# A two-block transformer kernel: the second block's projections token major from float32r parts, a shorter Fourier transform, modulation rows shared between engines, scores issued one unit further ahead

## The chip, the cores and the metric

One core of one Trainium2 chip runs the whole program. The metric is the device time of one execution in microseconds (us); lower is better. Before the change three runs took 1713.85, 1714.11 and 1716.21 us, median 1714.11.

## The reference, cut to what matters

256 tokens of width 1024 pass through a first block (attention, convolution, a mixture of 64 experts), then through a second block of two layers. The change touches the mixer of the second block's first layer:

```
xn   = rms_norm(h) * (1 + sc1) + sh1            # 256 x 1024
proj = xn @ w_in                                # 512 Fourier, 512 q, 128 k, 128 v columns
q, k = apply_rope(q), apply_rope(k)             # pairs (2j, 2j+1) turned by cos, sin of the position
attn = softmax(q k^T / 8 over window, context, sink) v
four = real(fft2(f_in, over tokens and over each head's 128 columns))
h    = h + g1 * (concat(four, attn) @ w_out)
h    = h + g2 * swiglu(rms_norm(h) * (1 + sc2) + sh2)
```

sh1, sc1, g1, sh2, sc2, g2 are six rows of 1024 of silu(c) @ ada_w + ada_b. The mixer needs rows 2 (g1), 3 (sh2) and 4 (sc2) while it runs; rows 0 and 1 were made in the first block. All inputs and outputs are f32.

## The kernel before, in words

Activations lie feature major: eight tiles of 128 features by 256 tokens. The first block ends with sixteen quads of experts, whose weights stream from memory. Weights pass through a ring of six slots of 2 MB (`wslot`, line 441), all issued on SP's queue in the order of the program.

The second block's mixer is built by `even` (line 1809). It issues the loads (kv2, late tables, q, f, modulation row 2, output weights, modulation rows 3 and 4), normalises with `norm_mod` (line 724), and then weaves four chains in a fixed order of preference: `attention2`, `gemvs2`, `projections`, `second_out`. `weave` (line 478) asks a model of the engines (`_Model`, line 271) when each chain's next piece can run, and lets the first chain that is ready put its instructions down; so the order on TensorE, VectorE and ScalarE is written out by the program. GpSimd's order is left to the scheduler. Every instruction passes through a helper, line 264, and so carries that line in the profile; the names of the tiles tell them apart.

- `projections` (line 1746): keys feature major, then values token major, then four query tiles and four Fourier tiles feature major, each eight f32 matmuls with 256 columns, stationary weights, moving tokens (`h`). After each key or query tile `rope` (line 1636) copies it (ScalarE), multiplies it with a swap matrix (TensorE) and combines with cos and sin (three VectorE operations).
- `fourier` and `dft` (lines 1651 and 1661): per head two matmuls with the 128-point cosines and sines for each of two token tiles, a copy, and four matmuls with the 256-point tables.
- `attention2` (line 1727): eight units (head pair i, query tile qt). `scores2` (line 1682) makes one unit's scores (`ps<-kall,qT`), subtracts from the mask with a running minimum (VectorE, reads PSUM), takes the exponential (ScalarE), and normalises half on VectorE and half on GpSimd. `attend2` (line 1707) turns the probabilities (`ps<-firstt,p`), copies them (ScalarE, `p2T`) and multiplies with the values (`ps<-p2T,vall`). Scores are issued one unit ahead: in turn u the scores of unit u + 1 are put down first, then the attending of unit u. The PSUM tags are of few banks: g 3, n 1, s 2, t 1, o 1.
- `gemvs2` (line 1770) makes modulation rows 2, 3 and 4 with `gemv` (line 639): on VectorE one multiply and seven multiply-adds of 1024 columns (`acc`), then four small matmuls with ones, a copy and two transposes.
- `second_out` (line 1777): the output projection, eight tiles of eight f32 matmuls; it waits for all projections, for modulation row 2 and for the first seven tiles of `mix`.

The feed-forward layers after it (`ffn_hidden`, line 1851) already work with parts: `split2` (line 1845) rounds a weight chunk to float32r on ScalarE (`whi`) and subtracts on VectorE or GpSimd (`wlo`), the activations are split too, and three float32r matmuls (high by high, high by low, low by high) stand for one in f32.

## Time and profile before

| | |
|---|---|
| median of three runs | 1714.11 us |
| the profiled execution's own time | 1714.49 us |
| its span, first to last instruction | 1712.7 us |
| mean granted TensorE clock | 0.897 of full speed |
| busy: TensorE, VectorE, ScalarE, GpSimd | 79%, 34%, 22%, 8% of the span |
| memory traffic | 589.49 MB, mean 344 GB/s |

The rows further below come from this one execution. Times in them are us from the span's start unless marked ns. A matmul in f32 is recorded as two instructions, one in float32r as one. `x16` is a count of instructions; the text in square brackets is the idle time of the engine just before, and what ended it. PE is TensorE, DVE VectorE, ACT ScalarE, POOL GpSimd.

### The profile page before, as it was taken

The page shows a single profiled execution, that of the slowest core. Times are in us where ns is not written, and L with a number is a line of the kernel's source. Part 1 is how long each engine was busy: PE and PEld are TensorE (multiplying, and loading weights), DVE is VectorE, ACT ScalarE, POOL GpSimd, SP SyncE. Part 2 cuts the span into 40 slices and gives each one's busy share as a digit, 9 for nine tenths or more (in the row PEclk, how much of TensorE's full clock was granted, in tenths as well). Part 3 has the DMA queues.
Part 4 walks back from the last instruction along what each step waited for, and adds up shares of the span by engine and source line. Part 5 has one row for each costly group of instructions (what it writes and reads, how often), then busy time and mean ns, then how long its engine had stood idle before and what let it go on. Part 6 is the DMA issues. An engine that isn't in the chain of part 4 may idle for free.

```text
span 1712.7 us, 18392 instructions
## 1 busy us (share of the span) xinstructions
PE 1348.3 (79%) x7664; PEld 782.8 (46%) x7664; DVE 575.8 (34%) x1109; ACT 375.6 (22%) x704; POOL 143.0 (8%) x80
## 2 busy tenths in 40 slices
PE   7999976665775765667666766769989999999997
PEld 5676832221221221222122212226667778778886
DVE  1567721110110111011011101115575878464533
ACT  2335110000000000100000000013324444554444
POOL 0000000000000000000000000002202232213224
PEclk9999998878888787888888778889999999999999
DMA  9787889999999999899999999996486786636620
GB/s 396 301 344 307 320 348 427 427 427 427 428 426 427 427 427 425 368 427 426 426 427 427 426 428 427 426 426 281 163 317 236 310 342 244 246 148 232 234 74 25
DMA packets 43994, 589.49 MB, mean 344 GB/s; under 512 B 4888, under 2 KB 5016, under 8 KB 7552
## 3 DMA queue, kind: packets, MB, share of 16 engines
q1 hardware_dynamic: 42768, 584.82, 82.5%
q0 software_dynamic: 704, 2.64, 0.4%
q8 instruction: 62, 1.02, 0.2%
q10 hardware_dynamic: 432, 0.79, 0.1%
q14 instruction: 28, 0.23, 0.0%
HBM read 587.16 MB, written 1.06 MB: 343 GB/s over the span
## 4 chain that ended last, share of the span: by engine, by line
PE 30%; DMA 24%; DVE 3%; ACT 1%; issue 1%; ACTq 0%; DVEq 0%
PE ps L264 30%; DMA w<-in_w 23%; DMA w<-in_w2last 1%; DVE acc L264 1%; DMA w<-in_ada 0%; DVE wlo L264 0%; DVE p L264 0%; ACT p L264 0%; DVE x L264 0%; DVE sqa L264 0%; ACT rstd L264 0%; DVE ada L264 0%; DVE mix L264 0%; ACT mix L264 0%; ACT sq L264 0%
## 5 line engine op out<-in xcount | busy, mean ns | idle before, releaser
L264 PE MATMUL ps<-w,xg 128*32 128x512 f32 x2016 | 301.3, 733 | 186.6 <-DMA w<-in_w 186.6
L264 PE MATMUL ps<-w,gT 128*32 128x512 f32 x1024 | 175.8, 821 | 104.9 <-DMA w<-in_w 96.9
L264 PEld LDWEIGHTS ps<-w,xg 128*32 128x32 f32 x2016 | 64.2, 122 | 404.7 <-DMA w<-in_w 209.8
L264 ACT ACTIVATE whi<-w 128x1024 fp32r<-128x1024 f32 x132 | 139.4, 1059 | 151.6 <-PE ps L264 146.0
L264 DVE TENSOR_TENSOR g<-g,ps 128x512 f32<-128x512 f32 x16 | 11.0, 687 | 458.1 <-PE ps L264 458.1
L264 DVE TENSOR_TENSOR wlo<-w,whi 128x1024 fp32r<-128x1024 f32 x88 | 114.7, 1311 | 111.6 <-ACT whi L264 111.4
L264 PE MATMUL ps<-whi,mix 128*128 128x512 f32 x352 | 140.1, 403 | 4.1 <-ACT mix L264 4.1
L264 DVE SCALAR_TENSOR_TENSOR acc<-w,sil,acc 128x1024 f32<-128x1024 f32 x98 | 141.8, 1447 | 2.6 <-DMA w<-in_ada 1.1
L264 POOL TENSOR_TENSOR wlo<-w,whi 128x1024 fp32r<-128x1024 f32 x44 | 112.6, 2570 | 349.9 <-ACT whi L264 293.0
L264 PE MATMUL ps<-wlo,mix 128*128 128x512 f32 x352 | 140.4, 400 | 0.0
L264 PE MATMUL ps<-whi,xl 128*128 128x512 f32 x352 | 138.5, 399 | 0.9 <-DVE xl L264 0.9
L264 PEld LDWEIGHTS ps<-w,gT 128*32 128x32 f32 x1024 | 32.9, 131 | 230.9 <-DMA w<-in_w 151.7
L264 DVE COPY y<-ps 128x512 f32<-128x512 f32 x16 | 11.1, 692 | 279.3 <-PE ps L264 279.3
L264 ACT ACTIVATE gT<-ps 128x512 f32<-128x512 f32 x16 | 9.6, 597 | 320.0 <-PE ps L264 320.0
L264 PE MATMUL ps<-hT,w 128*128 128x256 f32 x320 | 75.7, 383 | 2.4 <-DVE hT L264 2.4
L264 PEld LDWEIGHTS ps<-whi,mix 128*128 128x128 f32 x352 | 67.4, 192 | 22.1 <-ACT mix L264 5.3
L264 DVE SCALAR_TENSOR_TENSOR x<-ps,mod,x 128x256 f32<-128x256 f32 x152 | 67.2, 483 | 28.4 <-PE ps L264 28.4
L264 PEld LDWEIGHTS ps<-whi,xl 128*128 128x128 f32 x352 | 67.3, 191 | 16.6 <-DVE xl L264 1.7
L264 PEld LDWEIGHTS ps<-wlo,mix 128*128 128x128 f32 x352 | 67.5, 192 | 14.6 <-DVE wlo L264 0.4
L264 PE MATMUL ps<-wlo,gh 128*128 128x512 f32 x176 | 69.7, 399 | 0.0
L264 PE MATMUL ps<-oh,xtok 128*128 128x128 f32 x512 | 62.6, 283 | 8.7 <-DVE oh L264 8.7
L264 PE MATMUL ps<-whi,gl 128*128 128x512 f32 x176 | 69.2, 397 | 0.0
(304 smaller groups left out, 1497.5 us busy)
## 6 DMA issues: line engine op xcount, KB each, us to landing
w<-in_w SPq DMA_DIRECT2D x189, 2048.0 KB, 26.2
w<-in_ada SPq DMA_DIRECT2D x34, 2048.0 KB, 10.1
w<-in_f SPq DMA_DIRECT2D x32, 2048.0 KB, 8.3
w<-in_wout SPq DMA_DIRECT2D x4, 2048.0 KB, 8.6
w<-in_win SPq DMA_DIRECT2D x3, 2048.0 KB, 25.1
w<-in_conv SPq DMA_DIRECT2D x4, 1536.0 KB, 11.6
w<-in_ada1h SPq DMA_DIRECT2D x2, 2048.0 KB, 14.2
w<-in_cw SPq DMA_DIRECT2D x2, 2048.0 KB, 18.3
```

Of the source, the lines that this page charges most:

```text
L264: r = f(*args, **kw)
```

## The change

Six things change, all in the second block's first mixer.

1. The projections are token major: stationary token tiles, moving weights. Both are split into float32r parts: `norm_mod` writes a high and a low part of the input, `half` splits a weight chunk of 1024 columns (ScalarE the high part, VectorE and GpSimd half of the low part each), through four buffers of a pool that was there before. `tm_gemm` runs three float32r matmuls per token tile and 128 inputs. Keys and values come first, then all of q, then the Fourier input.
2. The rope works on token-major tiles without a swap matrix, then `turned` transposes keys and queries.
3. The Fourier transform takes the tokens first, with 129 cosine and 127 sine columns only, and makes the other half of the outputs from sums and differences.
4. `gemv_shared`: four of a modulation row's eight slices are scaled on ScalarE and added on GpSimd, four stay on VectorE; the matmuls with ones add both sums.
5. Scores are issued two units ahead.
6. The masks are fetched by GpSimd's DMAs instead of being copied from the late table, which shrinks from 1088 KB to 512 KB; the model's costs for float32r matmuls and GpSimd are lowered.

The core of the diff (the packing of the inputs and the tables are left out):

```diff
...
+    def half(self, w, c):
...
+        src = w[:, D * c:D * c + D]
+        hi, lo = [self.xtra.tile([P, D], F32R, tag="x", name=self.nm(n)) for n in ("whi", "wlo")]
+        nc.scalar.activation(hi, src, AF.Copy)
+        for eng, s in ((nc.vector, slice(0, 512)), (nc.gpsimd, slice(512, D))):
+            eng.tensor_tensor(lo[:, s], src[:, s], hi[:, s].bitcast(F32), ALU.subtract)
+        return hi, lo
...
+    def tm_gemm(self, ps, chunks, cols):
...
+        m = D // cols
+        for c in chunks:
+            yield from self.ahead_half(c + 1)
+            ws = self.halves[c]
+            for kk in range(m):
+                k = m * (c - chunks[0]) + kk
+                yield self.ready(ws[1][:, cols * kk:cols * kk + cols], self.hl[:, k, :])
+                for t in range(2):
+                    st = slice(P * t, P * t + P)
+                    hi, lo = [x[:, cols * kk:cols * kk + cols] for x in ws]
+                    self.mm(ps[t][:, :cols], lhsT=self.hh[:, k, st], rhs=hi, start=k == 0, stop=False)
+                    self.mm(ps[t][:, :cols], lhsT=self.hh[:, k, st], rhs=lo, start=False, stop=False)
+                    self.mm(ps[t][:, :cols], lhsT=self.hl[:, k, st], rhs=hi, start=False, stop=k == KT - 1)
+                yield self.clock
+            yield from self.ahead_half(c + 2)
...
+    def rope(self, src, t, scale):
...
+        q = self.wk(512, "ada")[:, :n]
+        nc.scalar.activation(q, src, AF.Copy, scale=scale)
+        r = self.ph(512, "rt", 1)[:, :n]
...
+        nc.vector.tensor_tensor(pairs(r), pairs(q)[:, :, :, ::-1], sin[:, None].to_broadcast([P, n // 64, 32, 2]), ALU.mult)
+        nc.vector.tensor_tensor(qh, qh, cos[:, None].to_broadcast([P, n // 64, 64]), ALU.mult)
+        nc.vector.tensor_tensor(q, q, r, ALU.add)
+        return q
...
+    def fourier(self, i, f):
...
         for t in range(2):
+            self.mm(pz[:, :S], lhsT=f[:, t, P * i:P * i + P], rhs=self.late("dft")[:, S * t:S * t + S],
+                    start=t == 0, stop=t == 1)
+        z = self.ph(S, "fz", 2)
+        nc.scalar.activation(z, pz[:, :S], AF.Copy)
...
+        self.mm(po[:, :129], lhsT=cs[:, :P], rhs=z[:, :129], start=True, stop=True)
+        self.mm(po[:, S:S + 127], lhsT=cs[:, P:], rhs=z[:, 129:], start=True, stop=True)
...
     def attention2(self):
...
-            for n in ((0, 1) if u == 0 else (u + 1,)):
+            for n in ((0, 1, 2) if u == 0 else (u + 2,)):
...
     def projections(self):
...
+        ps = yield from self.grab("g", 2)
+        yield from self.tm_gemm(ps, (0, 1), S)
+        k = []
+        for t in range(2):
+            nc.vector.tensor_copy(self.vall[:, 0, t, :], ps[t][:, P:S])
+            k.append(self.rope(ps[t][:, :P], t, 1.0))
...
+        ps = yield from self.grab("g", 2)
+        yield from self.tm_gemm(ps, (2, 3, 4, 5), 512)
+        q = [self.rope(ps[t], t, 0.125) for t in range(2)]
...
+        self.spawn(self.turned(q, [self.qT[:, :, P * t:P * t + P] for t in range(2)], [f"q{i}" for i in range(4)]))
+        ps = yield from self.grab("g", 2)
+        yield from self.tm_gemm(ps, (6, 7, 8, 9), 512)
...
+    def turned(self, src, outs, names):
+        for x, o in zip(src, outs):
+            yield self.ready(x)
+            yield self.room("n")
+            pt = self.ps("n")
+            n = o.shape[1]
+            for i in range(n):
+                self.tr(pt[:, P * i:P * i + P], x[:, P * i:P * i + P])
+            self.nc.vector.tensor_copy(o, pt[:, :P * n].rearrange("p (i s) -> p i s", i=n))
...
+    def gemv_shared(self, slots, c, bias, out):
...
+        t0 = yield from self.take(slots, 0)
+        for k in range(4):
+            nc.scalar.activation(t0[:, k, :], t0[:, k, :], AF.Copy, scale=c[:, k:k + 1])
+            yield self.model.clock["scalar"] - BACKLOG
+            if k % 2:
+                nc.gpsimd.tensor_tensor(t0[:, k - 1, :], t0[:, k - 1, :], t0[:, k, :], ALU.add)
+        nc.gpsimd.tensor_tensor(t0[:, 0, :], t0[:, 0, :], t0[:, 2, :], ALU.add)
+        t1 = yield from self.take(slots, 1)
+        acc = self.ph(D, "acc")
+        for k in range(4):
+            if k == 0:
+                nc.vector.tensor_scalar(acc, t1[:, 0, :], c[:, 4:5], None, ALU.mult)
+            else:
+                nc.vector.scalar_tensor_tensor(acc, t1[:, k, :], c[:, 4 + k:5 + k], acc, ALU.mult, ALU.add)
...
     def even(self):
...
+        self.halves = [self.half(self.ahead[n][0][1], i) for n, i in self.parts[:2]]
+        h = self.hh = self.ph(0, "h", shape=[P, KT, S], dt=F32R)
+        self.hl = self.ph(0, "hl", shape=[P, KT, S], dt=F32R)
         nc.gpsimd.memset(self.mask, 0.0)
-        nc.gpsimd.tensor_copy(self.mask[:, 0, P:2 * P], self.late("wm0"))
-        nc.gpsimd.tensor_copy(self.mask[:, 1, 0:P], self.late("wm1"))
+        nc.gpsimd.dma_start(self.mask[:, 0, P:2 * P], a["wm"][0])
+        nc.gpsimd.dma_start(self.mask[:, 1, 0:P], a["wm"][1])
...
+        self.norm_mod(self.x, self.scaled(self.v2("norm_mix_g_2", 0), self.m2(0, 1)), self.m2(0, 0),
+                      parts=(h, self.hl))
```

## Rows read from the trace of the kernel before

**Rows 1.** the chain that ended last: start us, us, engine, what

```profile
1121.89 25.00 DMA w<-in_w2last
...
1285.68 195.04 PE ps L264 x896
```

**Rows 2.** two stretches: busy us (instructions) by engine, clock, DMA share

```profile
1185.00:1246.00 61.00, 55.82 (x343) 39.97 (x342) 38.02 (x83) 20.60 (x54) 14.95 (x12) 0.97 0.42 158
1246.00:1276.00 30.00, 29.71 (x149) 24.46 (x147) 25.02 (x33) 7.26 (x13) 0.00 (x0) 1.00 0.80 310
```

**Rows 3.** TensorE's timeline, end of the mixer and start of the layer

```profile
1268.12 7.94 PE L264 MATMUL ps<-mix,w 128*128 128x256 f32 x36
...
1289.19 0.39 PE L264 MATMUL ps<-whi,mix 128*128 128x512 f32 x1
...
1289.42 0.39 PE L264 MATMUL ps<-wlo,mix 128*128 128x512 f32 x1
```

**Rows 4.** TensorE's groups by shape, 1156 to 1290 us: busy us, mean ns

```profile
L264 PE MATMUL ps<-h,w 128*128 128x256 f32 x144 | 36.8, 399 | 2.1 <-ACT h L264 2.1
...
L264 PE MATMUL ps<-mix,w 128*128 128x256 f32 x128 | 28.7, 381 | 0.0
...
L264 PE MATMUL ps<-latet,fz 128*128 128x256 f32 x32 | 7.9, 389 | 0.8 <-DVE fz L264 0.8
...
L264 PE MATMUL ps<-latet,ff 128*128 128x256 f32 x16 | 5.0, 438 | 0.5 <-ACT ff L264 0.5
...
L264 PE MATMUL ps<-w,h 128*128 128x128 f32 x32 | 4.4, 281 | 0.0
...
L264 PE MATMUL ps<-acc,cont 128*32 128x256 f32 x24 | 1.9, 390 | 0.3 <-DVE acc L264 0.2
```

**Rows 5.** timeline of the mixer's scaling; the page's group of weight conversions

```profile
1158.18 3.25 DVE L264 SCALAR_TENSOR_TENSOR nt<-x,mods,rstd 128x256 f32<-128x256 f32 x8 [2.17 <-ACT rstd L264]
...
L264 ACT ACTIVATE whi<-w 128x1024 fp32r<-128x1024 f32 x132 | 139.4, 1059 | 151.6 <-PE ps L264 146.0
```

**Rows 6.** two tiles, 1300 to 1700 us, ns min/median/max; timeline near 1410

```profile
L264 POOL TENSOR_TENSOR wlo<-w,whi x44: 2395/2410/3394, 1304.8 to 1692.9; 128x1024 fp32r<-128x1024 f32 x44
...
L264 DVE SCALAR_TENSOR_TENSOR acc<-w,sil,acc x42: 1276/1284/3319, 1335.1 to 1594.4; 128x1024 f32<-128x1024 f32 x42
...
1409.83 2.46 POOL L264 TENSOR_TENSOR wlo<-w,whi 128x1024 fp32r<-128x1024 f32 x1 [0.35 <-ACT whi L264]
...
1410.06 4.63 DVE L264 SCALAR_TENSOR_TENSOR acc<-w,sil,acc 128x1024 f32<-128x1024 f32 x2
```

**Rows 7.** timeline of attention: first scores and product, two periods, last product

```profile
1172.11 1.13 PE L264 MATMUL ps<-kall,qT 64*128 64x512 f32 x4
...
1181.79 1.09 PE L264 MATMUL ps<-p2T,vall 128*64 128x128 f32 x16
...
1199.93 1.13 PE L264 MATMUL ps<-kall,qT 64*128 64x512 f32 x4
...
1208.97 1.13 PE L264 MATMUL ps<-kall,qT 64*128 64x512 f32 x4
...
1212.55 0.57 ACT L264 ACTIVATE p2T<-ps 128x512 f32<-128x512 f32 x1
...
1213.18 0.66 PE L264 MATMUL ps<-firstt,p 128*128 128x128 f32 x4
...
1215.88 1.13 PE L264 MATMUL ps<-kall,qT 64*128 64x512 f32 x4
...
1239.49 1.10 PE L264 MATMUL ps<-p2T,vall 128*64 128x128 f32 x16
```

**Rows 8.** stretches of 3 us: busy us by engine, clock, DMA share

```profile
1159.00:1162.00 3.00, 2.74 (x7) 2.21 (x8) 2.44 (x7) 3.00 (x8) 0.00 (x0) 0.56 1.02 430
...
1216.00:1219.00 3.00, 1.59 (x8) 0.60 (x8) 1.84 (x6) 1.06 (x3) 0.00 (x0) 1.00 0.00 0
...
1222.00:1225.00 3.00, 3.00 (x21) 2.12 (x20) 2.16 (x4) 0.00 (x0) 0.80 (x1) 0.63 0.00 0
```

More of the change, by code (lines that the diff above doesn't have):

```diff
@@ L1563, in load_late @@
         nc = self.nc
-        self.latet = self.mid("latet")[:, :self.a["late"].shape[1]]
+        t = self.mid("latet")
+        self.mask = t[:, :D].rearrange("p (t k) -> p t k", t=2)
+        self.ff = t[:, D:2 * D].rearrange("p (t f) -> p t f", t=2)
+        self.latet = t[:, 2 * D:]
         d = nc.sync.dma_start(self.latet, self.a["late"])
@@ L1634, in context_kv @@
         self.done("kv")
-    def rope(self, out, ps, scale, name):
+    def half(self, w, c):
         nc = self.nc
-        q = self.ph(S, "rq", 2)
-        nc.scalar.activation(q, ps[:, :S], AF.Copy, scale=scale)
-        self.release(ps)
-        yield self.ready(q)
-        yield self.room("n")
-        pr = self.ps("n")
-        self.mm(pr[:, :S], lhsT=self.late("swap"), rhs=q, start=True, stop=True)
-        t = self.ph(S, "rt", 2)
-        nc.vector.tensor_tensor(t, pr[:, :S], self.late("sin"), ALU.mult)
-        nc.vector.tensor_tensor(q, q, self.late("cos"), ALU.mult)
-        nc.vector.tensor_tensor(out, q, t, ALU.add)
-        self.events[name] = True
@@ new lines, in half, with ahead_half @@
+        nc.scalar.activation(hi, src, AF.Copy)
+        for eng, s in ((nc.vector, slice(0, 512)), (nc.gpsimd, slice(512, D))):
+            eng.tensor_tensor(lo[:, s], src[:, s], hi[:, s].bitcast(F32), ALU.subtract)
+        return hi, lo
+    def ahead_half(self, n):
+        while len(self.halves) < min(n, len(self.parts)):
+            name, c = self.parts[len(self.halves)]
+            w = yield from self.take(name)
+            self.halves.append(self.half(w, c))
+    def tm_gemm(self, ps, chunks, cols):
[14 more added lines that the diff above has]
+            yield from self.ahead_half(c + 2)
@@ L1764, in projections @@
-        self.done("q")
-        for i in range(4):
-            yield from self.fourier(i)
-        self.done("f")
-        self.events["projections"] = True
+        ps = yield from self.grab("g", 2)
[4 more added lines that the diff above has]
+            k.append(self.rope(ps[t][:, :P], t, 1.0))
+        self.release(*ps)
+        self.done("kv2")
+        self.events["v"] = True
@@ new lines, in projections @@
+        f = self.ff
+        for t in range(2):
+            nc.scalar.activation(f[:, t, :], ps[t], AF.Copy)
+        self.release(*ps)
+        self.done("f")
+        yield self.ready(f)
+        for i in range(4):
+            yield from self.fourier(i, f)
+        self.events["projections"] = True
+    def turned(self, src, outs, names):
[7 more added lines that the diff above has]
+            self.nc.vector.tensor_copy(o, pt[:, :P * n].rearrange("p (i s) -> p i s", i=n))
+        for n in names:
+            self.events[n] = True
@@ L1772, in gemvs2 @@
         for i in (2, 3, 4):
-            o = 8 * i
-            yield from self.gemv(None, self.sil[:, 8:16], self.vec("ada_b_2")[:, o:o + 8], self.mod2[:, o:o + 8], f"ada2_{i}")
+            yield from self.gemv_shared(f"ada2_{i}", self.sil[:, 8:16], self.vec("ada_b_2")[:, 8 * i:8 * i + 8], self.mod2[:, 8 * i:8 * i + 8])
             self.events[f"ada2_{i}"] = True
+    def gemv_shared(self, slots, c, bias, out):
+        nc = self.nc
+        t0 = yield from self.take(slots, 0)
[12 more added lines that the diff above has]
+                nc.vector.scalar_tensor_tensor(acc, t1[:, k, :], c[:, 4 + k:5 + k], acc, ALU.mult, ALU.add)
+            yield self.model.clock["vector"] - BACKLOG
+        self.done(slots, 1)
+        yield self.ready(acc, t0[:, 0, :])
+        yield self.room("n")
+        ps = self.ps("n")
+        for n, src in enumerate((acc, t0[:, 0, :])):
+            for j in range(4):
+                self.mm(ps[32 * j:32 * j + 32, :S], lhsT=self.con("one1")[:, :32], rhs=src[:, S * j:S * j + S],
+                        start=n == 0, stop=n == 1, tile_position=(0, 32 * j))
+        self.done(slots, 0)
+        sb = self.wk(512, "ada")
+        nc.scalar.activation(sb[:, :S], ps[:, :S], AF.Copy)
+        yield self.ready(sb)
+        yield self.room("n")
+        pt = self.ps("n")[:, :S]
+        for q in range(2):
+            self.tr(pt[:, P * q:P * q + P], sb[:, P * q:P * q + P])
+        nc.vector.tensor_tensor(out.rearrange("p (j q) -> p q j", q=2), pt.rearrange("p (q j r) -> p q j r", q=2, j=4)[:, :, :, 0],
+                                bias.rearrange("p (j q) -> p q j", q=2), ALU.add)
+        yield self.clock
     def second_out(self):
```

101 lines of the change are left out of this document (37 added, 64 removed).

## The prediction, made before the change had run

> **What bounds the kernel now.** I read the chain of waits first, then the table of stretches, then the second block's mixer instruction by instruction. In the chain [rows 1] the experts' last weight transfer runs up to 1146.9 us; then comes the mixer, and from 1285.68 us 195 us of TensorE in the first feed-forward layer. The mixer stands in series with what follows, and the feed-forward layers are full of TensorE work, so every microsecond by which the mixer ends earlier or later reaches the end of the kernel. The stretches [rows 2] show two parts: from 1185 to 1246 us attention, the Fourier part and the rest of the projections (TensorE busy 55.8 of 61 us, VectorE 38.0, the DMA engines 42%), then to 1276 us the output projection, TensorE alone (29.7 of 30). No transfer holds the mixer. Its end is set by one of two things: the sum of TensorE's work, or the latency chain of the eight attention units. I cost both.
>
> **TensorE's work.** One f32 matmul is recorded as two instructions. 36 of them with 256 columns take 7.94 us, 0.216 each less the last one's latency; 512 columns of float32r start 0.23 us apart [rows 3]. The projections are 144 instructions of 256 columns and 32 of 128 [rows 4]: 144 x 0.216 + 32 x 0.108 = 34.6 us. The new ones are 48 instructions for keys and values (256 columns, half of 0.23, 5.5 us) and 48 each for queries and Fourier input (48 x 0.23 = 11.0): 27.5. Nothing in the trace shows float32r at 256 columns; the ends are 0.108 (half of 0.216) and 0.23 (no gain from fewer columns), 5.2 to 11.0 us. I take 0.115, since f32 at 128 columns also takes half of what it takes at 256. The five swap matmuls of 256 columns (10 x 0.216) give way to ten transposes (about 1.2 us): -1.0. The Fourier part goes from 48 x 0.216 = 10.4 us to four times 4 x 0.216 + 4 x 0.11 = 1.3, so 5.2. The modulation rows' reductions double, 8 instructions each, 3 x 0.63 = +1.9. In all TensorE loses 7.1 + 1.0 + 5.2 - 1.9 = 11.4 us. That would be the gain if TensorE's sum were all that counted.
>
> **When attention can start.** Before, the first scores start at 1172.11 us [rows 7], because query tile 0 is projected right after the keys. Now all of q comes before any score. *Keys and values:* the norm starts at 1158.18 [rows 5] and each of the eight input tiles now costs VectorE two instructions, the scaling and the low part (16 x 0.41 = 6.6 us, the row's eight take 3.25), so the last low part is there at 1164.9. TensorE begins there at a low clock, as it does now (0.56 from 1159 to 1162 us [rows 8]), so it falls behind; I put the end at 1167.3 (1166 to 1168.5). *Queries:* four chunks. With two pairs of buffers a chunk's conversion starts when TensorE has finished the chunk two before; it takes ScalarE 1.06 us [rows 5], then GpSimd's half of the low part, 1.2 us (half of 2.41 [rows 6]), with hops about 2.8, against 2.76 us of matmuls. I take 3.0 a chunk and 0.7 for the PSUM bank that the keys' rope still reads: end at 1180.0. *Rope and turning:* one more weight conversion stands ahead on ScalarE (1.06), then its copy (0.6), six VectorE operations of 512 columns at 0.64 (half of the modulation sum's 1.284 [rows 6]) make 3.8, then transposes and copies through a single bank, 2.2, and gaps of 0.8: 8.5 us. First scores at 1188.5 us, **+16.4** (from +14 to +20). Meanwhile TensorE has the Fourier input's 11 us, so it is the attention chain that moves.
>
> **How long attention takes.** Before, from 1172.11 to the end of the last unit at 1239.49 + 1.10 us, 68.5 us [rows 7]. One period [rows 7]: scores at 1208.97, the copy of transposed probabilities at 1212.55, the second transposes at 1213.18 after waiting for that copy, the next scores at 1215.88: 6.91 us. ScalarE takes the exponentials of the unit just scored before the copy of the older one. With scores two units ahead that order is the same, so depth does not shorten a period; it makes the first stretch one unit longer (about half a period, 3.5 us) and turns one long period at the end into a short one (3.7 us: two transposes of 0.66, two copies of 0.6, the product of 1.1). What shortens attention is that rope, projections and half the modulation sums are out of its way; before, the period that starts at 1199.93 us lasts 9.0. I take 15.0 for the first stretch (before, first scores to first product 10.8, plus 3.5, plus 0.7 for other work caught between), five periods of 6.9, two of 3.7: 56.9 us, **-11.6** (-14 to -3).
>
> **After attention.** Before, from 1240.6 to 1276.06 us [rows 3, 7], 35.5 us: the last of the Fourier part and all 128 instructions of the output projection [rows 4]. Now the Fourier part is done by then, and the output projection can start beside the last two units, which leave TensorE idle 1.3 us each: 128 x 0.216 = 27.6 - 2.6 + 0.3 for the last copy = 25.3, **-10.2** (-11 to -9).
>
> **Costed at nothing.** Two conversions among the squares at 1150 to 1157 us: ScalarE idles there between squares; without that cover 2.1 us. The masks: a memset and two DMA issues on GpSimd's queue instead of two copies, 20 us before the first score; behind them queue only low parts, 2.4 us if they came late. The late table is half as large and no one waits for it. SP's order of loads is the same; weight slots come free at conversion, not at the last matmul, so modulation rows and output weights are fetched earlier. The Fourier combination (small VectorE and ScalarE operations) lies beside attention. The third modulation row is needed only near 1265 us.
>
> **Sum.** +16.4 - 11.6 - 10.2 = -5.4 us on the profiled execution's 1714.49, so 1709.1; the median of the runs is 0.4 below the profiled one: **1708.7 us**.
>
> **Rival 1, the shared port makes it slower.** In the feed-forward layer a GpSimd subtraction starts at 1409.83 and lasts 2.46 us; a modulation sum that VectorE starts at 1410.06 ends only after it, and the longest such sum is 3.32 us against 1.28 [rows 6]. So a VectorE operation with two SBUF inputs stands still for the GpSimd operation, about 2.0 us. The Trainium skill (SBUF — State Buffer, "Who interferes with whom") calls the pair of ports an exclusive lock, held for the whole instruction; by that rule the trace agrees. The change puts nine GpSimd additions of 2.4 us beside attention, and ten GpSimd low parts of 1.2 us next to VectorE's low parts and rope. Against it: the score operation reads PSUM, and the deeper scores give slack behind normalisation. If four additions are caught on the chain (+8) and the ramp loses 3 us, the time is -5.4 + 11 = +5.6, 1720 us. It decides from about three collisions on, 5.4 / 2.0.
>
> **Rival 2, the clock eats the gain.** At 1216 to 1219 us TensorE was busy 1.59 of 3 us, and at 1222 to 1225 its granted clock was 0.63 of 2.4 GHz [rows 8], partly at 1.2. With the projections gone from attention's gaps, TensorE waits about 2.5 us a period for ScalarE. The Trainium skill (TensorE: Matmul & The Clock Gate, "HAM oscillation — how this bites in real kernels") says that bursts parted by waits pay the slow clock each time. A period at half clock loses 0.6 us on the second transposes and 1.1 on the product, 1.7. Two to five such periods give back 3.4 to 8.5: 1712 to 1717. Against it: Fourier pieces fill about four gaps.
>
> **Rival 3, nothing stands in the way.** Conversions at 2.76 us, short handovers (first scores at 1186, +13.9), a first stretch of 13.7, five periods of 6.7 and 7.0 at the end (54.2, -14.3), tail -10.5: -10.9, 1703.2 us.
>
> **Numbers.** Forecast 0.42, rival 1 0.21, rival 2 0.20, rival 3 0.17. A measurement of this kernel tells about 0.2%, 3.4 us, from no change. Faster: rival 3 and most of the forecast's spread, 0.53; the same: rival 2 and the forecast's slow edge, 0.22; slower: rival 1 and the worst of rival 2, 0.25. The range runs from rival 3 with 3 us more, 1700, to rival 1, 1720. The likeliest case alone spans 1705 to 1712.
>
> **What would show it.** Right: first scores near 1188 us of the span, periods near 7 us, the output projection's last matmul near 1271, the layers after it unchanged. Wrong: VectorE sums or rope operations of over 3 us beside GpSimd (rival 1), a granted clock well below 1 between 1195 and 1245 us (rival 2), or q chunks much over 3 us, which would mean that conversion and not TensorE sets the projections.

## The result, and the profile after

The changed kernel takes 1732.51 us (median of four runs, 1730.07 to 1735.51) against 1715.16 us beside it: ratio 1.0101, 95% interval 1.0081 to 1.0121. It is slower by 17.4 us, where 5.4 us less was forecast, and outside the range. The profiled execution's span is 1730.7 us against 1712.7.

All of the difference lies in the mixer. I cut each trace at five marks of its timeline: the copy of the experts' last output, the first scores, the end of attention's last product, the end of the output projection, the first feed-forward matmul (us, each number rounded by itself):

| stretch | before | forecast | after |
|---|---|---|---|
| experts' last output to first scores | 24.0 | 40.4 | 49.3 |
| attention | 68.5 | 56.9 | 68.3 |
| output projection | 35.5 | 25.3 | 30.0 |
| to the first feed-forward matmul | 6.6 | 6.6 | 4.5 |
| **the four together** | **134.5** | **129.2** | **152.1** |
| the layers after | 430.0 | 430.0 | 428.0 |

The four together are 17.5 us longer, which is the whole loss. Attention, which was to pay for the later start, is as long as before.

The timeline of the changed kernel, four stretches of it (columns as in [rows 3]):

```profile
1167.41 0.28 PE L260 MATMUL ps<-whi,h 128*128 128x256 f32 x1
1167.53 0.28 PE L260 MATMUL ps<-wlo,h 128*128 128x256 f32 x1
...
1183.48 0.69 DVE L260 TENSOR_TENSOR wlo<-w,whi 128x512 fp32r<-128x512 f32 x1 [2.11 <-ACT whi L260]
1183.53 1.79 POOL L260 TENSOR_TENSOR wlo<-w,whi 128x512 fp32r<-128x512 f32 x1 [1.01 <-ACT whi L260]
...
1186.76 0.69 DVE L260 TENSOR_TENSOR ada<-ada,rt 128x512 f32<-128x512 f32 x1
1187.00 1.61 POOL L260 TENSOR_TENSOR wlo<-w,whi 128x512 fp32r<-128x512 f32 x1 [1.68 <-ACT whi L260]
1187.56 1.60 DVE L260 TENSOR_TENSOR rt<-ada,latet 128x512 f32<-128x512 f32 x1
1187.97 0.60 PE L260 MATMUL ps<-firstt,ada 128*128 128x128 f32 x4
1189.07 7.86 POOL L260 TENSOR_TENSOR w<-w 128x1024 f32<-128x1024 f32 x3 [0.46 <-ACT w L260]
1189.19 2.78 DVE L260 TENSOR_TENSOR ada<-ada,latet 128x512 f32<-128x512 f32 x1
1192.00 2.71 DVE L260 TENSOR_TENSOR ada<-ada,rt 128x512 f32<-128x512 f32 x1
1195.37 1.12 PE L260 MATMUL ps<-firstt,ada 128*128 128x128 f32 x4 [6.80 <-DVE qT L260]
1199.96 1.75 PE L260 MATMUL ps<-kall,qT 64*128 64x512 f32 x4
...
1254.51 7.97 DVE L260 SCALAR_TENSOR_TENSOR acc<-w,sil,acc 128x1024 f32<-128x1024 f32 x3
1255.23 6.17 POOL L260 TENSOR_TENSOR w<-w 128x1024 f32<-128x1024 f32 x2
1262.40 0.41 DVE L260 COPY mix<-ps 128x256 f32<-128x256 f32 x1
1262.87 1.09 PE L260 MATMUL ps<-p2T,vall 128*64 128x128 f32 x16 [0.90 <-DVE mix L260]
...
1266.72 3.88 ACT L260 ACTIVATE whi<-w 128x1024 fp32r<-128x1024 f32 x4
...
1273.92 2.35 DVE L260 TENSOR_TENSOR wlo<-w,whi 128x1024 fp32r<-128x1024 f32 x2
1278.53 0.87 DVE L260 SCALAR_TENSOR_TENSOR x<-ps,mod,x 128x256 f32<-128x256 f32 x2
1279.06 19.22 PE L260 MATMUL ps<-mix,w 128*128 128x256 f32 x80 [3.71 <-DVE x L260]
```

Three things are to be seen. **Rope:** three rope operations of the first q tile took 0.69 us each (the last is at 1186.76); of the second, which ran beside a low part and then three additions on GpSimd, 1.60, 2.78 and 2.71. TensorE waits 6.8 us for that. In these rows it is the engine that starts later that is held up: at 1183.48 VectorE's low part began 0.05 us ahead of GpSimd's and took 0.69 us, as it does alone. **Sums:** three modulation sums on VectorE take 7.97 us beside two GpSimd additions, against 1.28 each alone [rows 6], and attention's own copy (`mix`) stands behind them until 1262.40. **The next layer's work:** ScalarE's four weight conversions and VectorE's low parts belong to the feed-forward layer, yet stand in the in-order queues ahead of the output projection's update of `x`, and TensorE idles 3.71 us.

Its stretches (columns as in [rows 2]: the span, then PE, PEld, DVE, ACT and POOL with counts, the clock, the DMA share and GB/s):

```profile
1162.00:1189.00 27.00, 23.48 (x114) 19.02 (x114) 17.88 (x34) 13.46 (x21) 9.93 (x6) 0.94 0.92 380
1189.00:1195.00 6.00, 0.00 (x0) 0.00 (x0) 5.93 (x4) 2.07 (x2) 5.85 (x3) 0.67 0.01 5
1195.00:1201.00 6.00, 5.01 (x14) 3.03 (x14) 3.74 (x4) 0.00 (x0) 1.93 (x1) 0.50 0.00 0
...
1200.00:1268.00 68.00, 55.65 (x357) 36.27 (x356) 47.08 (x104) 36.95 (x81) 39.45 (x24) 0.87 0.45 179
```

and attention in the kernel before:

```profile
1172.00:1241.00 69.00, 64.54 (x398) 46.11 (x397) 42.46 (x102) 24.90 (x66) 18.65 (x16) 0.98 0.45 177
```

After six empty microseconds TensorE's granted clock is 0.50 of 2.4 GHz, the lower level, and the first scores take 1.75 us instead of 1.13. In attention as a whole TensorE is busy 82% of the time at 0.87, where before it was busy 94% at 0.98: it lost work there, and the time did not shrink.

### The profile page after: what moved, and what is told of

Read it like the earlier page. It is cut to its first block, busy times and chain, and to the rows that moved or that the text cites. A ratio compares the mean times of both kernels' runs of the same rounds, so it can differ in the third digit from the quotient of the medians.

```text
span 1730.7 us, 18427 instructions
## 1 busy us (share of the span) xinstructions
PE 1351.4 (78%) x7640; PEld 781.0 (45%) x7640; DVE 590.4 (34%) x1125; ACT 398.7 (23%) x727; POOL 184.5 (11%) x99
## 4 chain that ended last, share of the span: by engine, by line
PE 30%; DMA 23%; DVE 4%; ACT 2%; issue 1%; ACTq 0%; DVEq 0%
PE ps L260 30%; DMA w<-in_w 23%; DVE acc L260 1%; DVE p L260 1%; DVE wlo L260 1%; ACT p L260 1%; DVE ada L260 1%; ACT whi L260 0%; DVE x L260 0%; ACT rstd L260 0%; DVE p2st L260 0%; DVE nt L260 0%; DVE rt L260 0%; ACT mix L260 0%; ACT p2T L260 0%
## 5 line engine op out<-in xcount | busy, mean ns | idle before, releaser
L260 ACT ACTIVATE whi<-w 128x1024 fp32r<-128x1024 f32 x142 | 149.9, 1058 | 158.4 <-PE ps L260 154.5
L260 POOL TENSOR_TENSOR wlo<-w,whi 128x1024 fp32r<-128x1024 f32 (+1 forms) x54 | 128.1, 2382 | 411.7 <-ACT whi L260 350.2
L260 DVE TENSOR_TENSOR wlo<-w,whi 128x1024 fp32r<-128x1024 f32 (+1 forms) x98 | 125.9, 1293 | 124.8 <-ACT whi L260 124.7
L260 DVE SCALAR_TENSOR_TENSOR acc<-w,sil,acc 128x1024 f32<-128x1024 f32 x86 | 132.5, 1541 | 1.4
L260 PE MATMUL ps<-whi,gl 128*128 128x512 f32 x176 | 69.5, 397 | 0.0
## 6 DMA issues: line engine op xcount, KB each, us to landing
w<-in_conv SPq DMA_DIRECT2D x4, 1536.0 KB, 11.3
```

The lines of the kernel that those rows point to most:

```text
L260: r = f(*args, **kw)
```

## The experiments

All results in one table: the median, its ratio to the kernel before measured beside it, and the stretches cut as above (us, one profiled execution each, each number rounded by itself).

| run | median | ratio, 95% interval | to scores | attention | output | to layer | four together |
|---|---|---|---|---|---|---|---|
| before | 1714.8 to 1715.5 | | 24.0 | 68.5 | 35.5 | 6.6 | 134.5 |
| after | 1732.51 | 1.0101 (1.0081 to 1.0121) | 49.3 | 68.3 | 30.0 | 4.5 | 152.1 |
| a_gemv | 1723.66 | 1.0052 (1.0035 to 1.0069) | 42.5 | 65.8 | 29.0 | 6.8 | 144.1 |
| a_lodve | 1728.54 | 1.0073 (1.0055 to 1.0092) | 43.0 | 71.1 | 29.9 | 4.5 | 148.5 |
| a_nopool | 1721.83 | 1.0039 (1.0026 to 1.0051) | 40.8 | 68.7 | 27.4 | 6.7 | 143.6 |
| b_gemv | 1720.52 | 1.0033 (1.002 to 1.0046) | 24.0 | 69.5 | 43.8 | 4.4 | 141.7 |
| a_depth1 | 1731.74 | 1.0102 (1.0085 to 1.0119) | 48.8 | 66.0 | 34.8 | 4.5 | 154.2 |
| a_later | 1730.51 | 1.0094 (1.0078 to 1.0111) | 41.7 | 67.0 | 35.8 | 5.0 | 149.4 |
| a_tail | 1731.62 | 1.0105 (1.0089 to 1.0122) | 48.4 | 70.2 | 24.4 | 10.8 | 153.8 |
| b_four | 1703.97 | 0.9945 (0.9929 to 0.9962) | 22.3 | 61.8 | 34.7 | 4.4 | 123.3 |
| b_four2 | 1705.88 | 0.995 (0.9937 to 0.9962) | 22.3 | 61.8 | 34.7 | 4.4 | 123.3 |
| b_order | 1707.27 | 0.9959 (0.9947 to 0.9971) | 35.9 | 61.1 | 26.0 | 6.5 | 129.5 |
| a_nopool_d1 | 1712.51 | 0.9987 (0.9978 to 0.9996) | 41.4 | 63.4 | 26.1 | 4.4 | 135.3 |
| a_halfq | 1716.56 | 1.0009 (1.0 to 1.0018) | 31.1 | 70.4 | 29.9 | 5.3 | 136.8 |
| b_four_d2 | 1713.01 | 0.9991 (0.9979 to 1.0004) | 22.3 | 68.4 | 35.3 | 6.9 | 132.8 |
| a_gemv_d1 | 1718.41 | 1.0018 (1.0008 to 1.0028) | 42.0 | 63.0 | 26.1 | 4.4 | 135.5 |
| a_halfq_d1 | 1717.66 | 1.0014 (1.0002 to 1.0026) | 32.3 | 71.1 | 32.2 | 5.9 | 141.5 |

b_four and b_four2 are the same kernel: their four stretches agree to 0.1 us, while their spans differ by 5.0 (1699.0 and 1704.0), of which 3.2 lies in the layers after. So the last column compares two profiled executions more sharply than their spans do. It does not stand for the median, though: the median less the last column runs from 1576.1 us (a_halfq_d1) to 1583.0 (a_gemv_d1, whose profiled execution was the fastest of its ten). Where a difference is small, both are given.

### GpSimd's share: a_gemv, a_lodve, a_nopool

a_gemv: modulation rows made on VectorE alone, as before.

```diff
-            yield from self.gemv_shared(f"ada2_{i}", ...)
+            yield from self.gemv(None, ..., f"ada2_{i}")
```

> The changed kernel with the modulation rows made as before, all eight slices on VectorE, and no GpSimd additions. Theory (shared port): the three additions from 1189 to 1197 us no longer stop the queries' rope (6.8 us of TensorE waiting) and six later ones no longer stop the sums (about 10 us in all, 1.4 to 2 us each); the twelve extra VectorE multiply-adds of 1.28 us give some of it back. Time 1732 - 17 + 4, so 1717 to 1721. Rival (the late start of attention, all of q before any score, is the cause): the first scores stay near 1200 us and the time stays above 1727.

a_lodve: low parts on VectorE alone.

```diff
-        for eng, s in ((nc.vector, slice(0, 512)), (nc.gpsimd, slice(512, D))):
+        for eng, s in ((nc.vector, slice(0, D)),):
```

> The changed kernel with the low parts of the second block's projection weights all on VectorE (1024 columns, 1.13 us) instead of half on GpSimd. Theory (shared port): the low halves cost 1.8 us each on both engines now, so VectorE alone is no slower; the conversions come 0.5 us sooner each, 1728 to 1732; the additions remain and hold the rope. Rival (the low halves are the main blocker): 1722 or less.

a_nopool: both edits.

> Both edits: nothing of the change is left on GpSimd but the masks, normalisation stays as it was. Theory (shared port): the forecast's sum without collisions holds apart from the extra VectorE work, 1712 to 1718, first scores near 1191 us of the span. Rival (late start): above 1725.

GpSimd's new work costs 152.1 - 143.6 = 8.5 us of the mixer, 1732.51 - 1721.83 = 10.7 us of the time. Added to a_nopool by itself, the low parts cost 0.5 us of the mixer (a_gemv; 1.8 in the medians) and the modulation rows 4.9 (a_lodve; 6.7). Without GpSimd the second q tile's rope takes 0.69 us an operation, where my sum had 0.64 (timeline of a_nopool, the last two of its operations):

```profile
1185.90 0.69 DVE L260 TENSOR_TENSOR ada<-ada,latet 128x512 f32<-128x512 f32 x1
1186.63 0.69 DVE L260 TENSOR_TENSOR ada<-ada,rt 128x512 f32<-128x512 f32 x1
```

and its first scores come 30.0 us after the norm's start, against 30.3 in my sum (1188.5 - 1158.18). But 9.1 us above the kernel before remain (143.6 - 134.5), with attention at 68.7 us: GpSimd is about half of the loss (8.5 of 17.5 us in the mixer, 10.7 of 17.4 in the medians). Of the three expectations, a_lodve's came out in its range of time, though VectorE's low halves take 0.7 us in five of ten cases and not the 1.8 that it went by. The other two held for the start of attention (scores at 1189.5 and 1190.9 us, where the rival of a_gemv had them near 1200), while the times, 1723.66 and 1721.83 us, lie between theory and rival: part of the loss was not GpSimd's.

### The shared modulation rows in the kernel before: b_gemv

```diff
+    def gemv_shared(self, slots, c, bias, out):
...
-            yield from self.gemv(None, ..., f"ada2_{i}")
+            yield from self.gemv_shared(f"ada2_{i}", ...)
```

> The kernel before with one part of the change alone: modulation rows shared between ScalarE, GpSimd and VectorE. Theory (shared port): nine additions of 2.4 us stand beside rope (three short operations per tile, spread out) and sums; two to four of them are caught on the chain, 4 to 8 us slower, 1719 to 1723. Rival (the additions only hurt where the whole rope stands in one lump behind the queries): within 3 us of before, or faster, since VectorE loses 15 us of sums.

The mixer grows by 7.2 us: the output stage is 8.3 us longer (43.8 against 35.5). There (timelines of the kernel before, then of b_gemv) ScalarE's conversions for the next layer now come ahead of the copy that the last modulation row waits for:

```profile
1267.06 0.38 ACT L264 ACTIVATE ada<-ps 128x256 f32<-128x256 f32 x1
1267.34 3.88 ACT L264 ACTIVATE whi<-w 128x1024 fp32r<-128x1024 f32 x4
```

```profile
1270.69 3.88 ACT L264 ACTIVATE whi<-w 128x1024 fp32r<-128x1024 f32 x4
1274.48 0.36 ACT L264 ACTIVATE ada<-ps 128x256 f32<-128x256 f32 x1
...
1274.89 0.69 PE L264 MATMUL ps<-firstt,ada 128*128 128x128 f32 x2 [2.73 <-ACT ada L264]
```

This wait is 2.7 of the 8.3 us. Another 2.6 are Fourier work left over when attention ended (the output projection's first instruction comes 7.9 us after attention instead of 5.3), and the last 36 instructions take 9.18 us instead of 7.94 [rows 3], the granted clock from 1275 to 1285 us being 0.86. The time, 1720.52 us, is in the theory's range, but by luck: the theory had the additions caught on the chain, and the first scores come as before (24.0), with attention 1.1 us longer. So edit 4 costs in either kernel, in different places: here a row that is late holds up the output stage.

### Later modulation rows: a_later

```diff
     def gemvs2(self):
-        yield self.event("q1")
+        yield self.event("mix4")
```

> The chain of modulation rows starts only after the first Fourier head is done (an event later than q1), so that GpSimd's three additions of about 2.4 us are no longer beside the rope of q; everything else as changed. Theory (rope's three VectorE operations standing still for GpSimd's additions are the loss of the ramp): from the norm to the first scores 30 to 33 us instead of 38.5, TensorE's gap of 6.8 us ahead of the turning of q shrinks to under 3, and the time falls by 4 to 8 us, to 1724.5 to 1728.5 us, unless the additions then collide with attention's normalisation. Rival A (the additions only move: the rows come due later and hold up attention or the output stage by as much): ramp as short, but attention or output longer, 1730 us or more. Rival B (rope is late for another reason, conversions or the order on ScalarE): ramp 37 us or more.

The timeline of a_later:

```profile
1184.85 1.59 DVE L260 TENSOR_TENSOR rt<-ada,latet 128x512 f32<-128x512 f32 x1
1186.47 0.69 DVE L260 TENSOR_TENSOR ada<-ada,latet 128x512 f32<-128x512 f32 x1
1187.20 0.69 DVE L260 TENSOR_TENSOR ada<-ada,rt 128x512 f32<-128x512 f32 x1
...
1267.09 6.87 PE L260 MATMUL ps<-mix,w 128*128 128x256 f32 x18 [4.04 <-DVE x L260]
```

The two operations that had stood still for the additions are back at 0.69, and the first scores come 31.3 us after the norm instead of 38.5: the additions made that wait. (mix4 is set by the first unit pair of attention, not, as the expectation says, by a Fourier head.) Rival A of the expectation describes the rest: the rows come due later and the output stage is 5.7 us longer, so the time falls by 2.0 us only.

### The next layer's work held back: a_tail

```diff
+        d = nc.scalar.activation(hi, src, AF.Copy)
+        self.tc.add_manual_dep(d.ins, self.x_done.ins.name, ...)
...
+        d = nc.vector.tensor_scalar(acc, t[:, 0, :], c[:, 0:1], None, ALU.mult)
+        self.tc.add_manual_dep(d.ins, self.x_done.ins.name, ...)
```

The first of these is in `split2`, for its first four weights, the second in `gemv`, for the first sum.

> The first four weight conversions of the feed-forward layer (ScalarE) and the first sum of its modulation row (VectorE) wait for the mixer's last update of x; nothing else changes. Theory (these operations, put into the in-order queues ahead of the output stage's own, make TensorE's idle time of 3.7 us in the output projection): the idle time goes, from the last product of attention to the end of the output projection 26 to 27.5 us instead of 30.0, the layer starts up to 2 us later after the mixer's end since its first weights are converted later; time 1727 to 1731.5 us. Rival (the output stage is late for the modulation row or the last mix tiles): output stage 29 us or more, and the layer's start 2 us later, 1732.5 us or more.

The timeline of a_tail:

```profile
1265.50 24.44 PE L260 MATMUL ps<-mix,w 128*128 128x256 f32 x112
...
1295.04 3.49 DVE L260 TENSOR_TENSOR wlo<-w,whi 128x1024 fp32r<-128x1024 f32 x3
1298.44 1.28 DVE L260 SCALAR_TENSOR_TENSOR acc<-w,sil,acc 128x1024 f32<-128x1024 f32 x1
1299.64 1.27 DVE L260 SCALAR_TENSOR_TENSOR nt<-x,mods,rstd 128x256 f32<-128x256 f32 x3
1300.71 0.79 PE L260 MATMUL ps<-whi,mix 128*128 128x512 f32 x1 [8.30 <-ACT mix L260]
```

The idle time goes and the output stage takes 24.4 us, within 1 us of my forecast. But the low parts and sums now stand ahead of the layer's norm, TensorE waits 8.3 us there, and the layer starts 6.3 us later after the output projection (10.8 against 4.5), where the expectation had up to 2; the time is the same. Held back in this way, the work only moves; it had a price of nothing in my sum.

### Depth of the scores: a_depth1, a_nopool_d1, a_gemv_d1, b_four_d2

a_depth1, the changed kernel one unit ahead; a_nopool_d1 and a_gemv_d1 make the same edit on a_nopool and a_gemv; b_four_d2 makes its reverse on b_four.

```diff
-            for n in ((0, 1, 2) if u == 0 else (u + 2,)):
+            for n in ((0, 1) if u == 0 else (u + 1,)):
```

> Edit 5 undone alone: scores one unit ahead again. My prediction gave depth no effect on a period (6.9 us either way) and only moved half a period from the end of attention to its start. Theory (GpSimd, the clock and the order of the in-order queues make the loss, depth is neutral): the first stretch becomes some 3.5 us shorter, the last periods longer by as much, attention stays at 66 to 70 us and the time within 4 us of the changed kernel, 1728.5 to 1736.5 us. Rival A (depth harms: the third unit's work in the first stretch delays the first product and with it everything): attention 64 us or less, 1727 us or less. Rival B (depth is what keeps the pace: normalisation late behind the shared port is hidden by it): attention over 71 us, 1737 us or more.

> The changed kernel with the modulation rows and the low parts on VectorE alone (edits 4 and half of 1 undone) and scores one unit ahead (edit 5 undone): what is left is the float32r token-major projections with all of q first, the new rope, and the short Fourier transform. Beside the kernel with the Fourier edit alone (1703.97 us) it gives the price of the projections' edit. Theory (projecting all of q, with conversions and rope, before any score takes TensorE's work out of attention, where it lay beside the latency chain, and puts it ahead in series): norm to first scores 29 to 31 us against 12.2, attention 63 to 68 us against 61.8, TensorE busy under 85% of attention; time 1718 to 1724 us, so the projections' edit costs 14 to 20 us. Rival (the loss was GpSimd and the depth, and the projections are neutral or gain): 1710 us or less.

> The changed kernel with the modulation rows on VectorE alone (1723.66 us) and the scores one unit ahead; GpSimd keeps half of the low parts. Theory (depth costs by itself, and undoing it in the changed kernel was hidden only by the order of the output stage): attention 61 to 64 us instead of 65.8, time 1713 to 1719 us. Rival (depth costs only where GpSimd has none of the low parts either): 1720 us or more.

> The kernel before with the Fourier edit alone (1703.97 and 1705.88 us), scores two units ahead; nothing else. Theory (depth delays the first product by a unit and returns little of it at the end, because the drain of the last units takes 4 to 6.5 us each and not 3.7): first stretch longer by 3 to 7 us, the end shorter by 1 to 3; the time up by 2 to 6 us, 1707 to 1711 us. Rival (depth is free where TensorE has other work to fill the stretch): attention 60 to 63 us as now (61.8), 1702 to 1707 us.

With two units ahead the mixer is longer by 8.3 us (a_nopool over a_nopool_d1), 8.7 (a_gemv over a_gemv_d1) and 9.6 (b_four_d2 over b_four); in the medians by 9.3, 5.3 and 7.1 to 9.0. Attention itself has 5.3, 2.8 and 6.5 us of it; about 2.4 us each time lie between the output projection and the layer. a_depth1 shows no gain for a reason of its own (its timeline):

```profile
1270.71 0.75 DVE L260 TENSOR_SCALAR acc<-w,sil 128x1024 f32<-128x1024 f32 x1 [5.84 <-DMA w<-in_ada]
...
1274.92 0.86 DVE L260 SCALAR_TENSOR_TENSOR x<-ps,mod,x 128x256 f32<-128x256 f32 x2
1275.45 20.55 PE L260 MATMUL ps<-mix,w 128*128 128x256 f32 x80 [9.05 <-DVE x L260]
```

Attention is 2.3 us shorter there, but VectorE then waits at the head of its queue for the DMA of the next layer's modulation row, with the update of `x` behind it: TensorE idles 9.05 us instead of 3.71.

What depth does is plainest in the kernel with the least else in it. b_four_d2, then b_four (timelines):

```profile
1182.10 1.13 PE L265 MATMUL ps<-kall,qT 64*128 64x512 f32 x4
1183.16 0.66 PE L265 MATMUL ps<-firstt,p 128*128 128x128 f32 x4
...
1188.42 1.09 PE L265 MATMUL ps<-p2T,vall 128*64 128x128 f32 x16
```

```profile
1177.46 0.60 PE L265 MATMUL ps<-firstt,p 128*128 128x128 f32 x4
...
1181.47 1.09 PE L265 MATMUL ps<-p2T,vall 128*64 128x128 f32 x16
```

The third unit is of the second head pair; its scores must wait until query tile 1 is projected and has its rope, and the first unit's transposes, put down after them, wait along. The first product ends 18.8 us after the first scores instead of 10.8, and of these 8.0 us attention's end gets 1.5 back (68.4 against 61.8). In a_nopool, where all of q is there, the first product ends at 19.5 us instead of 13.4 and attention's end comes 5.3 later.

Of the expectations, a_gemv_d1's theory came out. b_four_d2's was right in kind and too small (8.0 us ahead instead of 3 to 7, 1713.01 us instead of at most 1711). a_depth1's time lies in the range of "depth is neutral", which the other three pairs contradict. a_nopool_d1's put the price of the projections at 14 to 20 us; it is 12.0 in the mixer and 6.6 to 8.5 in the medians, between theory and rival.

### The Fourier edit alone: b_four, b_four2

The kernel before with edit 3, the Fourier input token major in f32.

```diff
-        for i in range(4):
-            yield from self.fourier(i)
+        for t in range(2):
+            ps = yield from self.grab()
+            for k in range(KT):
+                self.mm(ps, lhsT=self.hT[:, k, P * t:P * t + P], rhs=w[:, k, :], start=k == 0, stop=k == KT - 1)
...
+        for i in range(4):
+            yield from self.fourier(i, f)
```

> Edit 3 alone on the kernel before: the Fourier input token major (f32, moving weights of 512 columns), tokens first with 129 cosine and 127 sine columns, the other half of the outputs from sums and differences; projections, rope, modulation rows and depth as before. Theory (the Fourier edit alone was worth its 5.2 us of TensorE's work, because before most of that work stood after attention; what lost was GpSimd, the late q and the order of the queues): ramp 13.9 us and attention 66 to 69 us as before, output stage 30 to 32 us instead of 35.5, 1708 to 1712 us. Rival A (TensorE's sum is not what sets the end, the attention chain is): 1713.5 to 1717 us. Rival B (the combination's VectorE operations and the order of the queues cost more than they give): 1717.5 us or more.

> The kernel before with the Fourier edit alone, again, for a narrower interval. 1701 to 1707 us, 8 to 14 us below the kernel before. If it falls within 3.4 us of the kernel before, the first measurement of it was chance.

This kernel is the fastest of all: 10 us below the one before. It is also some 4 us below what the expectation of b_four had at best. My sum had 5.2 us of TensorE's work for the edit; the mixer loses 11.3: 1.7 ahead of the scores, 6.6 in attention, 0.8 in the output stage and 2.2 before the layer. The stretch of attention (b_four):

```profile
1172.00:1234.00 62.00, 58.70 (x353) 35.83 (x352) 41.81 (x105) 25.42 (x67) 18.69 (x16) 1.00 0.58 222
```

TensorE is busy 95% of attention at full clock; before, it was 94% at 0.98. Work taken from it there came off the time. That twice 5.2 us comes off has at least one other reason, in the 1.7 us ahead of the scores (timelines of the kernel before and of b_four, the same sixteen instructions after the same wait, then a stretch of b_four beside the first of [rows 8]):

```profile
1159.26 5.41 PE L264 MATMUL ps<-h,w 128*128 128x256 f32 x16 [2.07 <-ACT h L264]
...
1160.62 3.72 PE L265 MATMUL ps<-h,w 128*128 128x256 f32 x16 [2.07 <-ACT h L265]
...
1160.00:1163.00 3.00, 2.38 (x11) 2.05 (x12) 2.80 (x8) 2.94 (x8) 0.00 (x0) 1.00 1.05 444
```

The granted clock was at 1.00 there in b_four and at 0.56 before, though the instructions are the same. The sixteen take 3.72 us in all four executions that have the Fourier edit alone or with one line more (b_four, b_four2, b_four_d2, b_order) and 5.41 in the two without it (before, b_gemv); why was not found. In the 2.2 us before the layer TensorE waits 1.64 us for VectorE's sum of squares instead of 3.33. What is left, 7.4 us against 5.2, was not taken apart; the edit also moves copies between VectorE and ScalarE, so it is not TensorE's work alone.

### q first: b_order, a_halfq, a_halfq_d1

b_order: b_four, with the first scores waiting for the last query tile.

```diff
         yield self.event("k")
+        yield self.event("q3")
```

> The kernel before with the Fourier edit alone (1703.97 us), and one line more: the first scores wait until the last query tile is projected and turned; same matmuls, same rope, nothing on other engines. It moves three query tiles (48 instructions of 0.216 us, 10.4 us, and three swap matmuls) ahead of attention, and leaves it the Fourier part alone as filler. Theory (the order alone costs, because TensorE then waits for the latency chain): ramp 24 to 27 us instead of 12.2, attention 55 to 60 us instead of 61.8, TensorE's share in attention down from 95% to under 88%, time up by 5 to 12 us, to 1709 to 1716 us. Rival (attention shrinks by what leaves it, since TensorE's sum bounds both): ramp and attention together 74 to 76 us as now, 1702 to 1707 us; then the conversions and the new rope, not the order, are the price of the projections' edit.

```profile
1187.00:1248.00 61.00, 54.73 (x330) 32.17 (x330) 45.90 (x110) 25.42 (x68) 19.82 (x16) 0.97 0.57 212
```

(b_order's attention.) The scores come 13.6 us later than in b_four, attention shrinks by 0.8 only, with TensorE down to 90% busy, and the output stage gets 8.7 back, since the Fourier part is done early enough for 24 of the output projection's instructions to lie in attention's last gaps. In all the mixer is 6.3 us longer; the medians differ by 1.4 to 3.3 us, less than either the theory's 5 or the mixer's 6.3, and beside b_four2, measured along with it, the two intervals overlap. So the mixer shows a price for the order, the medians hardly do. The rival, that attention shrinks by what leaves it, falls; the theory's size is too large.

a_halfq: a_nopool with q in two halves of 256 columns; a_halfq_d1: the same, one unit ahead.

```diff
-        yield from self.tm_gemm(ps, (2, 3, 4, 5), 512)
-        q = [self.rope(ps[t], t, 0.125) for t in range(2)]
+        for j in range(2):
+            ps = yield from self.grab("g", 2)
+            yield from self.tm_gemm(ps, (2 + 2 * j, 3 + 2 * j), S)
+            q = [self.rope(ps[t][:, :S], t, 0.125) for t in range(2)]
```

> As the changed kernel without GpSimd in the modulation rows and the low parts (1721.83 us), but q is projected in two halves of 256 columns (heads 0 to 3, then 4 to 7), with rope and turning after each, so that attention can start after the first half and the second lies beside it. Float32r at 256 columns starts a matmul every 0.118 us in the changed kernel's key and value part, so the halves cost TensorE the same. Theory (q first is what costs): norm to first scores 21 to 25 us instead of 30.0, attention 65 to 70 us as TensorE's work moves into it, and the time falls by 4 to 9 us, to 1713 to 1718 us. Rival (attention lengthens by what the ramp wins, since its chain shares ScalarE and VectorE with the second half's conversions and rope): attention 73 us or more, 1719 us or more.

> q in two halves, no GpSimd in the modulation rows and low parts, scores one unit ahead: with two units ahead 1716.56 us. Theory (depth and q first are separate prices): from the experts' last output to the first feed-forward matmul 128 to 132 us instead of 136.8, time 1706 to 1712 us; that would put the float32r projections at about the price of the f32 ones (123.2 us of that stretch with the Fourier edit alone) and show that they can't win beside attention, since their conversions and rope share ScalarE and VectorE with it. Rival A (the prices overlap): 1713 us or more. Rival B (with both undone the 7.1 us less of TensorE's work shows): under 1704 us, the fastest kernel here.

Half of q first wins 9.7 us ahead of the scores and 5.3 of the time, as its theory had it, and attention grows by 1.8. Together with depth one the gain does not add (1717.66, rival A). The longest period of a_halfq_d1 is the one after its first product, 12.2 us. In it VectorE goes without a pause from 1193.88 us through two sums, a low part and the second half's six rope operations before it comes to the third unit's scores at 1200.30, as the rival of a_halfq has it: an attention that shares its engines with the second half. Which of its other waits (an idle time of 2.04 us for the update of `x` again, a period of 9.7 us in the middle of attention) would come back in another order stays open.

## Why the prediction was wrong, step by step

One path from before to after, each step a run, in us of the mixer and in medians: the Fourier edit -11.3 (1704 to 1706), the float32r projections with q first +12.0 (1712.5), depth +8.3 (1721.8), GpSimd +8.5 (1732.5); together +17.5. On another path the shares would differ, as a_depth1 shows. The second step (scores 19.1 us later, attention 1.6 longer, output stage 8.6 shorter) holds edits 1, 2 and 6 together; b_order and a_halfq test the order of q, but no run has the new rope, the masks or the model's lower costs alone.

- **TensorE's work** was sized rightly where rows show it: float32r at 256 columns starts a matmul every 0.12 us (1167.41 to 1167.53; I took 0.115).
- **"When attention can start"** failed in its rope and turning: 8.5 us in the sum, 14.6 measured, with 2.1 more before it. Without GpSimd the whole step holds, term by term (from the norm's start: keys and values 8.8 us against 9.1, queries 22.1 against 21.8, scores 30.0 against 30.3); with it the scores come at 38.5. Two conversions among the squares, which I put at nothing, made the norm start 0.7 us later. Rival 1's mechanism came true here: a VectorE operation that started after GpSimd's ended 0.55 us after it (1189.16 and 1188.61), and the last sum 1.08 us after the second addition (1262.48 and 1261.40); alone the two take 0.69 and 1.28 us. The Trainium skill (SBUF — State Buffer, "Who interferes with whom") has the rule that whoever issues first holds the shared ports and the other is blocked; these rows follow it. I gave the rival 0.21, with 3 us for the ramp; it took 7.2 (a_later) to 8.5 (a_nopool). Its whole price, 11 us above the forecast, is near the 10.7 that the medians show for GpSimd. What no rival held is the rest, 1721.83 against 1708.7 us without GpSimd's new work.
- **"How long attention takes"** is the step that failed most: 56.9 forecast, 68.3 measured, and 68.7 without any of GpSimd's new work. *First stretch:* 19.0 us against 15.0; three units, the sums and the Fourier input's conversions share ScalarE and VectorE there, partly at half clock, and no run parts these. *Depth:* I put its price at 3.5 us ahead; it is 3.3 (a_depth1), 6.1 (a_nopool), 6.5 (a_gemv) and 8.0 (b_four). I put its return at 6.4 (two periods of 3.7 at the end); the last two took 6.5 and 4.3 us. But one unit ahead ends with a short period as well (4.3 in a_nopool_d1), so that over the same four pairs only 1.0 to 1.9 us come back. *Periods:* an undisturbed one is 6.6 to 6.9, as I put it, but two of the five are 9.6 and 8.8; in a_nopool two are 8.2 and 8.6, so GpSimd's new work alone doesn't make them.
- **"After attention"**: 25.3 forecast, 30.0 measured, 24.4 in a_tail. The step counted TensorE's instructions only; the next layer's conversions and sums, of which the list of what costs nothing has no word, stand ahead of `x` in the queues, and in a_tail came back as 6.3 us before the layer. The order alone can pull them forward: they start 22.6 us after attention's end in b_four, 4.8 after it in b_order.
- **Rival 2** is right in its mechanism: 0.50 from 1195 to 1201 us after a wait of 6.8, 0.87 over attention, 0.86 in a_nopool. The Trainium skill (TensorE: Matmul & The Clock Gate, "HAM oscillation — how this bites in real kernels") has bursts that are parted by waits pay for the slow clock; these rows agree. No run prices the clock over attention by itself, so that rival's size stays open.
- **The frame:** I asked which of two things sets the end, TensorE's sum or attention's chain, and then let the gains of both add. The work of q stood beside the chain; put in front of it, it delays the scores in full (13.6 us in b_order, of which 8.7 come back at the other end), and the chain hardly shortens (0.8).

## What to carry to other kernels

Before you put work that lies beside a latency chain in front of it, ask whether the chain gets shorter: here it hardly did (scores 13.6 us later, attention 0.8 shorter), and only 8.7 us came back behind it. Where an engine was 95% busy beside the chain, cutting its work gave more. Before giving GpSimd half of an operation with two SBUF inputs, list what VectorE does in those microseconds: here its rope operations and sums that started after GpSimd's ended only after them. When a stage gets shorter or its order changes, look at what the scheduler pulls into the in-order queues from the next stage, up to a sum that waits for a DMA with the critical update behind it.

## What the runs showed that I had not expected

- A 0.69 us operation on VectorE takes 2.7 to 2.8 us beside a GpSimd addition of 1024 columns, and GpSimd's additions stretch as well, from 2.36 us alone to 2.62 each (7.86 for three) beside rope and 3.1 (6.17 for two) beside the modulation sums.
- The layers after the mixer took 426.3 and 429.5 us in two executions of one kernel (b_four, b_four2). Set side by side, the two differ in two places, by 1.7 us each, and in both places it is TensorE's granted clock. One of them (timelines of b_four, then b_four2):

```profile
1477.42 7.17 PE L265 MATMUL ps<-w,mix 128*128 128x256 f32 x32 [2.07 <-ACT mix L265]
...
1480.79 8.86 PE L265 MATMUL ps<-w,mix 128*128 128x256 f32 x32 [2.07 <-ACT mix L265]
```

  After the same wait of 2.07 us the same instructions ran at 1.00 in one (1478.5 to 1480.3 us) and at 0.54 in the other (1481.7 to 1485). Why it fell in the one only was not found.
- Doing one thing more in series (b_order) moved the mixer by 6.3 us and the median by a quarter to a half of it.
